# Starting the squared middle tiles and the block-product weights a few bytes into their SBUF buffers

## The chip, the cores and the metric

The kernel runs on one core of one Trainium2 chip. The metric is the device time of one execution, in microseconds. Before the change it is 1267.39 us, the median of three runs that lie between 1266.71 and 1267.39 us. One further execution was profiled, and every duration below comes from that one.

## The reference

The reference is a decoder trunk of two layers over 512 positions and 1024 channels, in float32. Each layer mixes positions with three parallel head groups (differential attention, a short gated convolution, RWKV-7) and then runs a squared-ReLU MLP. The change lies in the MLP alone:

```python
h = rms_norm(x, norm_mlp_g[l])
x = x + jnp.square(jax.nn.relu(h @ w_mlp_up[l])) @ w_mlp_down[l]
```

Here `w_mlp_up[l]` is 1024 x 4096 and `w_mlp_down[l]` is 4096 x 1024. After the last layer there is one more RMSNorm.

## The kernel before

Activations are held transposed: 128 channels on the partitions, 512 positions along the free dimension, so that one tile is 128 x 512 float32, 2048 bytes in each partition. Eight tiles make up the residual `x`.

To keep float32 accuracy with the fast `float32r` matmuls, every operand is split into a rounded part `hi` and a rest `lo`, and each product is made of three matmuls: `hi` by `hi`, `hi` by `lo` and `lo` by `hi`. ScalarE writes each `hi`, VectorE or GpSimd subtracts to get each `lo`. TensorE therefore issues, for each k of 128 channels, three weight loads and three matmuls. In a matmul the 128 x 128 weights are the operand that is loaded ahead (the stationary one), and the 128 x 512 or 128 x 256 activations are streamed through (the moving one).

The layer runs in stages. The first is the mixing stage, whose order of instructions is written out by hand; its last part, the output projection (`po` in the profile), takes `mhi` and `mlo` as moving operands. The second is the MLP, which lies in the `fp` pool of the layer and is emitted in plain program order:

- `up(i)` for the first 8 of 32 groups of middle channels (three of them are already done in the mixing stage): 24 matmuls of 512 columns each.
- `two(i0, i1)`, called 12 times a layer, does the other 24 groups in pairs by a scheme with 7 block products in the place of 8. Each product has 4 steps of k with 3 matmuls of 256 columns: 84 matmuls a call. The weights come as `raw` tiles or as their sums `s1` to `s4`, and `both` splits them into `shi` and `slo`, five buffers of each.
- `square` applies ReLU and the square, and `kept` splits the result into the middle tiles `mh` (ScalarE, line 1376) and `ml` (GpSimd, line 1377). They stand in rings of ten buffers each.
- `down(h, js)` multiplies four middle tiles by the down weights: for each output tile j, 12 matmuls of 512 columns with `mh` and `ml` as moving operands (`dn` in the profile). Between two calls of `two` stands half of such a group, 48 matmuls.
- In layer 1 the last quarter of the down projection is `last_group` (`dnF` in the profile): five output tiles with 24 matmuls of 512 columns, and three output tiles in two halves of 256 columns.

A matmul has two gates: its weights must be loaded and its moving operand written. The rings set how far ahead the other engines may work, and TensorE takes its work strictly in the order of the program.

Where tiles stand in a partition matters for what follows. The allocator rounds each buffer to a multiple of 32 bytes. In the program before, all middle tiles, all `shi` and `slo`, and the `thi`, `tlo`, `bhi` and `blo` activations start at a multiple of 64 bytes; the first middle tile, for example, at byte 98176. In the output projection the tiles are not all placed alike. The channel blocks are taken in the order 0, 5, 3, 1 (first four steps of `K_ORD`), and blocks 0 and 5 live in the mixing stage's own pool (`OWN`), while 3 and 1 live in the constant pool:

| moving tile of `po` | start byte in layer 0 | in layer 1 | past a multiple of 64 |
|---|---|---|---|
| `mhi`, `mlo` of block 0 | 210336, 212384 | 218528, 220576 | 32 |
| `mhi`, `mlo` of block 5 | 216480, 218528 | 212320, 214368 | 32 |
| `mhi`, `mlo` of block 3 | 35712, 37760 | 35712, 37760 | 0 |
| `mhi`, `mlo` of block 1 | 27520, 29568 | 27520, 29568 | 0 |

So each output tile of that projection's first part begins with six matmuls whose moving operand starts 32 bytes off, followed by six at a multiple of 64. Two kinds of weights are placed differently in the same way: `ksq`, the weights of the small `phsk` matmuls (128 x 128 weights, two columns streamed), stands 32 bytes off for the first two head pairs of layer 0 and at a multiple of 64 for the third.

A few elementwise outputs already start off a 32-byte multiple: `p[:, 1:]` at line 784 begins 4 bytes into its tile, `dx` written at line 906 starts 4 bytes past a multiple of 64, and `z[:, 2:]` at line 1220 begins 8 bytes into its tile.

Of the kernel before, what the change touches and what calls it, by code (L numbers as in the profile page):

```python
# [10 lines left out]
F32 = mybir.dt.float32  # L11
F32R = mybir.dt.float32r
# [10 lines left out]
S = 512  # L23
P = 128
# [255 lines left out]
def tile_trunk(ctx: ExitStack, tc: tile.TileContext, xT, wts, prm_d, cst_d, lora_d, gup_d, lam_d, fin_d, out):  # L280
# [25 lines left out]
    def psum(tag, bufs, name):  # L306
        return ps.tile([P, 512], F32, tag=tag, bufs=bufs, name=name)
# [177 lines left out]
    def last_group(fp, wbase, mids):  # L485


        g, H = N_KG - 1, S // 2
        mine = mids[8 * g:8 * g + 8]
# [18 lines left out]
        def norm(half, sq):  # L508
            q = slice(half * H, (half + 1) * H)
            pt = psum("rp", 4, f"pssF{half}")  # L510
            for i, a in enumerate((acc[:, q], sq)):
                for b in range(2):

                    pe.matmul(pt[:, b:b + 1], a[:, b * P:(b + 1) * P], ones1, start=(i == 0 and b == 0), stop=True,
                              skip_group_check=True)
            r = cp.tile([P, NB], F32, tag="rr", bufs=2, name=f"rrF{half}")
            for _ in rsqrt_act_steps(r[:, :2], pt[:, :2], 2, 1.0 / D, EPS):
                pass
            yield

            rb = [psum("rp", 4, f"prbF{half}_{i}") for i in range(1 + half)]
            for p in rb:
                for b in range(2):
                    pe.matmul(p[:, b * P:(b + 1) * P], r[:, b:b + 1].to_broadcast([P, P]), ident, start=True, stop=True)
            rbs = fp.tile([P, H], F32, tag="c0", bufs=2, name=f"rbs{half}")
            act.copy(rbs, rb[-1][:, :H])
            os_ = []
            for j in range(NK):
                o = fp.tile([P, H], F32, tag=("p1", "p5", "u2", "c1")[j // 2], bufs=2, name=f"o{half}_{j}")
                if j == 5 or j == 2 and not half:  # L530
                    pool.tensor_tensor(o, x[j][:, q], rbs, ALU.mult)
                else:
                    dve.tensor_tensor(o, x[j][:, q], rb[0][:, :H], ALU.mult)
                os_.append(o)
            for j in (0, 1, 3, 4, 2, 6, 5, 7):
                (nc.scalar if half and j in (1, 4, 6, 7) else nc.sync).dma_start(ov[j][:, q], os_[j])
            yield
# [34 lines left out]
    for l in range(L):  # L572
# [790 lines left out]
        with ExitStack() as mx:  # L1363
            fp = mx.enter_context(tc.tile_pool(name=f"fp{l}", bufs=1))
            RING = 10
            H = S // 2
            mids = []

# [2 lines left out]
            def kept(m):  # L1371

                i = len(mids)
                hi = fp.tile([P, S], F32R, tag="mh", bufs=RING, name=f"mh{l}_{i}")
                lo = fp.tile([P, S], F32R, tag="ml", bufs=RING, name=f"ml{l}_{i}")
                act.copy(hi, m)  # L1376
                pool.tensor_tensor(lo, m, hi.bitcast(F32), ALU.subtract)  # L1377
                mids.append((hi, lo))

            def square(cs, name):  # L1380

                r = fp.tile([P, S], F32, tag="r", bufs=2, name=f"r{name}")
                for i, c in enumerate(cs):
                    act.activation(r[:, i * H:i * H + c.shape[1]], c, AF.Relu)
                m = fp.tile([P, S], F32, tag="m", bufs=3, name=f"m{name}")
                act.activation(m, r, AF.Square)
                kept(m)
# [14 lines left out]
            bn, th = {}, {}  # L1402

            def scaled_by_norm(j):
                bn[j] = fp.tile([P, 2, H], F32, tag="shi" if j < 5 else "slo", bufs=5, name=f"bn{l}_{j}")
                dve.scalar_tensor_tensor(bn[j].rearrange("p a s -> p (a s)"), x[j], pr[:, C_GMLP + j:C_GMLP + j + 1], rb,
                                         ALU.mult, ALU.mult)

# [22 lines left out]
            def two(i0, i1):  # L1431

                n = f"{l}_{i0}"
                wg = wbase + NG_IN + NG_OUT

                def raw(i, a):
                    t = fp.tile([P, 4, P], F32, tag="sraw", bufs=6, name=f"raw{n}_{i}_{a}")
                    nc.sync.dma_start(t.rearrange("p k c -> p (k c)"), wts[wg + i, :, a * P:(a + 4) * P])
                    return t

                def both(src, name):
                    hi, lo = [fp.tile([P, 4, P], F32R, tag=f"s{p}", bufs=5, name=f"s{p}{n}_{name}") for p in ("hi", "lo")]
                    act.copy(hi, src)  # L1443
                    dve.tensor_tensor(lo, src, hi.bitcast(F32), ALU.subtract)  # L1444
                    return hi, lo

                def sum_(name, a, b, op):
                    t = fp.tile([P, 4, P], F32, tag=name, name=f"{name}{n}")
                    dve.tensor_tensor(t, a, b, op)
                    return t  # L1450

                def small(name):
                    return fp.tile([P, H], F32, tag=name, bufs=2, name=f"{name}{n}")

                def product(pt, w, moving, first=True):

                    whi, wlo = w
                    for k in range(4):
                        ahi, alo = moving(k)
                        pe.matmul(pt, whi[:, k], ahi, start=(first and k == 0), stop=False, skip_group_check=True)  # L1460
                        pe.matmul(pt, whi[:, k], alo, start=False, stop=False, skip_group_check=True)
                        pe.matmul(pt, wlo[:, k], ahi, start=False, stop=(k == 3), skip_group_check=True)

                blk = lambda d, q: lambda k: [p[:, q] for p in bs[4 * d + k]]
                smm = lambda q: lambda k: [p[:, q] for p in th[k]]
                pa, pb = [psum("rp", 4, f"p{i}{n}")[:, :H] for i in "ab"]
                pc = psum("at", 2, f"pc{n}")[:, :H]
                c0 = fp.tile([P, S], F32, tag="c0", bufs=2, name=f"c0{n}")
                w11 = raw(i0, 0)
                product(pa, both(w11, "p1"), blk(0, 0))  # L1470
                p1 = small("p1")
                act.copy(p1, pa)
                w21 = raw(i1, 0)
                w22 = raw(i1, 4)
                s1 = sum_("s1", w21, w22, ALU.add)
                product(pb, both(s1, "p5"), smm(0))
                p5 = small("p5")
                dve.tensor_copy(p5, pb)
                s2 = sum_("s2", s1, w11, ALU.subtract)
                product(pa, both(s2, "p6"), smm(1), False)  # L1480
                u2 = small("u2")
                act.copy(u2, pa)
                w12 = raw(i0, 4)
                product(pc, both(w12, "p2"), blk(1, 0))
                dve.tensor_tensor(c0[:, :H], pc, p1, ALU.add)
                s3 = sum_("s3", w11, w21, ALU.subtract)
                product(pa, both(s3, "p7"), smm(2), False)
                c1 = small("c1")
                dve.tensor_tensor(c1, pa, p5, ALU.add)  # L1489
                s4 = sum_("s4", w12, s2, ALU.subtract)  # L1490
                product(pb, both(s4, "p3"), blk(1, 1), False)
                dve.tensor_tensor(c0[:, H:], pb, u2, ALU.add)
                square([c0], f"{n}_0")
                product(pa, both(w22, "p4"), smm(3), False)
                square([pa, c1], f"{n}_1")
# [14 lines left out]
            for i in range(N_ONE):  # L1510
                up(i)
                for j in range(2 * max(i - 2, 0), min(2 * max(i - 1, 0), NK)):
                    scaled_by_norm(j)
                if i >= N_ONE - 4:
                    blocks(i - N_ONE + 4)
# [79 lines left out]
```

## Time and profile before

| what | value |
|---|---|
| median of three runs | 1267.39 us |
| the profiled execution's own time | 1266.47 us |
| its span, first to last instruction | 1264.7 us |
| TensorE matmul busy | 1242.8 us, 98% |
| VectorE, ScalarE, GpSimd busy | 72%, 55%, 27% |
| granted TensorE clock | 0.998 |
| matmuls `dn` (down projection), 512 columns | 3 x 448 |
| matmuls `dnF`, 512 and 256 columns | 3 x 40 and 3 x 48 |
| matmuls `pa`, `pb`, `pc` (block products), 256 columns | 2016 |

In the timeline each matmul has a start and a duration. The duration holds the whole trip through the array and overlaps with the next matmul's, so the cost of one matmul in a dense stream is read from the distance between successive starts, not from its duration. The windows view gives each engine's busy time in a stretch of the span, and the chain view lists the work that ended last, in order of time.

### The profile page before, as it was taken

The numbers are of one execution on the slowest core, as the hardware profiler recorded it, in microseconds if no ns is written. First come the engines' busy times: TensorE is split into PE (matmuls) and PEld (weight loads), VectorE is DVE, ScalarE is ACT, GpSimd is POOL, SyncE is SP. The second block draws the span as 40 slices with busy tenths as digits, with TensorE's granted clock in tenths as the row PEclk, the third lists the DMA queues.
The fourth block names the chain that finished last, engine by engine and source line by source line (L and its number), as shares of the span: only waits on it lengthen the run. The fifth ranks groups of instructions, "written<-read, shape, count | busy, mean of one in ns | idle before, by whom it ended". The sixth has DMA issues, their size and how long they took to land.

```text
span 1264.7 us, 25145 instructions
## 1 busy us (share of the span) xinstructions
PE 1242.8 (98%) x9493; PEld 1051.4 (83%) x9493; DVE 913.5 (72%) x1889; ACT 696.9 (55%) x1474; POOL 335.3 (27%) x433
## 2 busy tenths in 40 slices
PE   9999999999999999999999999999999999999997
PEld 6777777787789898989878787787787989898987
DVE  6788888867966666765667787879598666666654
ACT  7675655646744544544575656564575545454553
POOL 1353626133300101010224335352431010111110
PEclk9999999999999999999999999999999999999999
DMA  6522333142333333321235333332424233333122
GB/s 212 159 84 94 109 94 101 52 134 83 103 122 101 101 101 100 101 84 51 75 103 146 98 102 110 98 97 60 134 92 133 93 107 96 106 98 103 59 74 77
DMA packets 84410, 127.93 MB, mean 101 GB/s; under 512 B 21440, under 2 KB 25024, under 8 KB 84288
## 3 DMA queue, kind: packets, MB, share of 16 engines
q1 hardware_dynamic: 83568, 125.77, 32.6%
q8 instruction: 75, 1.23, 0.4%
q10 hardware_dynamic: 720, 0.55, 0.1%
q14 instruction: 47, 0.39, 0.1%
HBM read 117.11 MB, written 9.18 MB: 100 GB/s over the span
## 4 chain that ended last, share of the span: by engine, by line
PE 70%; DVE 4%; issue 1%; ACT 1%; DMA 0%; POOL 0%; DVEq 0%; ACTq 0%; POOLq 0%
PE dn L289 22%; PE pj L289 11%; PE pa L289 11%; PE up L289 6%; PE pb L289 5%; PE po L289 4%; PE dnF L289 3%; PE pc L289 3%; PE sc L289 1%; PE ptt L294 1%; PE pg L289 1%; DVE wlo L343 0%; DVE blo L1429 0%; DVE x L1505 0%; PE pyy L289 0%
## 5 line engine op out<-in xcount | busy, mean ns | idle before, releaser
L1377 POOL TENSOR_TENSOR ml<-m,mh 128x512 fp32r<-128x512 f32 x64 | 95.2, 1489 | 510.8 <-ACT mh L1376 510.6
L342 ACT CAST whi<-raw 128x512 fp32r<-128x512 f32 x142 | 88.1, 621 | 174.1 <-PE dn L289 158.5
L289 PE MATMUL dn<-mh,whi 128*128 128x512 f32 x448 | 175.3, 391 | 1.9 <-DVE x L1505 1.9
L289 PE MATMUL dn<-ml,whi 128*128 128x512 f32 x448 | 174.6, 390 | 0.0
L289 PE MATMUL dn<-mh,wlo 128*128 128x512 f32 x448 | 174.4, 389 | 0.0
L289 PE MATMUL pj<-ahim,whi 128*128 128x512 f32 x392 | 157.7, 402 | 4.4 <-DVE vf L1266 1.7
L289 PE MATMUL pj<-ahim,wlo 128*128 128x512 f32 x392 | 158.3, 404 | 0.0
L289 PE MATMUL pj<-alom,whi 128*128 128x512 f32 x392 | 158.2, 404 | 0.0
L662 ACT CAST whi<-raw 128x512 fp32r<-128x512 f32 x142 | 87.7, 619 | 93.6 <-PE pj L289 40.4
L671 POOL TENSOR_TENSOR wlo<-raw,whi 128x512 fp32r<-128x512 f32 x62 | 81.7, 1317 | 214.5 <-ACT whi L662 198.3
L1505 DVE TENSOR_TENSOR x<-dn,x 128x512 f32<-128x512 f32 x112 | 76.8, 686 | 76.8 <-PE dn L289 76.8
L343 DVE TENSOR_TENSOR wlo<-raw,whi 128x512 fp32r<-128x512 f32 x142 | 115.2, 812 | 11.4 <-ACT whi L342 10.7
L1444 DVE TENSOR_TENSOR slo_p<-s,shi_p 128x512 fp32r<-128x512 f32 x96 | 70.9, 740 | 63.6 <-ACT shi_p L1443 58.9
L289 PEld LDWEIGHTS dn<-mh,whi 128*128 128x128 f32 x448 | 84.2, 188 | 21.3 <-ACT whi L342 2.4
L289 PEld LDWEIGHTS dn<-mh,wlo 128*128 128x128 f32 x448 | 84.1, 188 | 17.8
L289 PEld LDWEIGHTS dn<-ml,whi 128*128 128x128 f32 x448 | 84.2, 188 | 16.5
L289 PEld LDWEIGHTS pj<-ahim,whi 128*128 128x128 f32 x392 | 73.9, 188 | 19.8 <-issue 1.7
L1443 ACT CAST shi_p<-s 128x512 fp32r<-128x512 f32 x96 | 59.2, 618 | 51.2 <-PE pa L289 39.1
L289 PEld LDWEIGHTS pj<-ahim,wlo 128*128 128x128 f32 x392 | 73.8, 188 | 14.3 <-issue 0.9
L289 PEld LDWEIGHTS pj<-alom,whi 128*128 128x128 f32 x392 | 73.8, 188 | 14.1 <-issue 0.5
L289 PE MATMUL pa<-thi,shi_p 128*128 128x256 f32 x288 | 81.6, 283 | 0.2 <-DVE c L1489 0.2
L289 PE MATMUL pa<-thi,slo_p 128*128 128x256 f32 x288 | 81.5, 283 | 0.0
(409 smaller groups left out, 3264.5 us busy)
## 6 DMA issues: line engine op xcount, KB each, us to landing
raw<-wts SPq DMA_DIRECT2D x391, 256.0 KB, 2.7
qs<-dqhi SPq DMA_DIRECT2D x24, 128.0 KB, 3.3
ks<-dkhi SPq DMA_DIRECT2D x24, 128.0 KB, 3.8
x<-xT SPq DMA_DIRECT2D x8, 256.0 KB, 5.0
dqhi<-qhi SPq DMA_DIRECT2D x6, 256.0 KB, 3.3
dqlo<-qlo SPq DMA_DIRECT2D x6, 256.0 KB, 2.8
dkhi<-khi SPq DMA_DIRECT2D x6, 256.0 KB, 2.6
dklo<-klo SPq DMA_DIRECT2D x6, 256.0 KB, 2.9
```

The costliest lines, as they stand in the source:

```text
L289: ins = nc.tensor.matmul(*a, **k)
L294: ins = nc.tensor.transpose(*a, **k)
L342: act.copy(hi[:, :n], raw[:, :n])
L343: (pool if a and lean[0] else dve).tensor_tensor(lo[:, :n], raw[:, :n], hi[:, :n].bitcast(F32), ALU.subtract)
L662: yield act.copy(hi[:, k0:k1], raw[:, k0:k1])
L671: yield eng.tensor_tensor(lo[:, :n], raw[:, :n], hi[:, :n].bitcast(F32), ALU.subtract)
L1377: pool.tensor_tensor(lo, m, hi.bitcast(F32), ALU.subtract)
L1443: act.copy(hi, src)
L1444: dve.tensor_tensor(lo, src, hi.bitcast(F32), ALU.subtract)
L1505: dve.tensor_tensor(x[j], pt, x[j], ALU.add)
```

## The change

The buffers of `mh`, `ml`, `shi`, `slo` and `bn` (which shares the buffers of `shi` and `slo`) grow from 512 to 544 elements, 128 bytes more in each partition. The middle tiles then use the 512 elements from element 4 (16 bytes) in layer 0 and from element 2 (8 bytes) in layer 1. The split block weights use those from element 4 (16 bytes) in layer 0 and from element 12 (48 bytes) in layer 1. `bn` still starts at element 0. No instruction is added or removed, no operand changes its shape, and the order stays the same. Because the larger buffers are all a multiple of 128 bytes longer, every other tile of the pool keeps its start relative to a multiple of 64.

```diff
             RING = 10
+            FROM, MID_FROM = ((4, 4), (12, 2))[l]
...
-                hi = fp.tile([P, S], F32R, tag="mh", bufs=RING, name=f"mh{l}_{i}")
-                lo = fp.tile([P, S], F32R, tag="ml", bufs=RING, name=f"ml{l}_{i}")
+                hi = fp.tile([P, S + 32], F32R, tag="mh", bufs=RING, name=f"mh{l}_{i}")[:, MID_FROM:MID_FROM + S]
+                lo = fp.tile([P, S + 32], F32R, tag="ml", bufs=RING, name=f"ml{l}_{i}")[:, MID_FROM:MID_FROM + S]
...
-                bn[j] = fp.tile([P, 2, H], F32, tag="shi" if j < 5 else "slo", bufs=5, name=f"bn{l}_{j}")
+                bn[j] = fp.tile([P, S + 32], F32, tag="shi" if j < 5 else "slo", bufs=5,
+                                name=f"bn{l}_{j}")[:, :S].rearrange("p (a s) -> p a s", s=H)
...
-                    hi, lo = [fp.tile([P, 4, P], F32R, tag=f"s{p}", bufs=5, name=f"s{p}{n}_{name}") for p in ("hi", "lo")]
+                    hi, lo = [fp.tile([P, S + 32], F32R, tag=f"s{p}", bufs=5,
+                                      name=f"s{p}{n}_{name}")[:, FROM:FROM + S].rearrange("p (k c) -> p k c", c=P) for p in ("hi", "lo")]
```

## The prediction

> **What bounds the kernel now.** I read the page first, from its busy times to the chain of work that ended last, then the windows of the two MLP stages, then the chain inside one of them, and last the timeline of single matmuls.
>
> ```profile
> PE 1242.8 (98%) x9493; PEld 1051.4 (83%) x9493; DVE 913.5 (72%) x1889; ACT 696.9 (55%) x1474; POOL 335.3 (27%) x433
> ...
> PE 70%; DVE 4%; issue 1%; ACT 1%; DMA 0%; POOL 0%; DVEq 0%; ACTq 0%; POOLq 0%
> PE dn L289 22%; PE pj L289 11%; PE pa L289 11%; PE up L289 6%; PE pb L289 5%; PE po L289 4%; PE dnF L289 3%; PE pc L289 3%; PE sc L289 1%; PE ptt L294 1%; PE pg L289 1%; DVE wlo L343 0%; DVE blo L1429 0%; DVE x L1505 0%; PE pyy L289 0%
> ```
>
> TensorE carries the chain, and the down projection (`dn`, `dnF`) and the block products (`pa`, `pb`, `pc`), whose operands the change moves, are its largest parts. The windows say whether anything else limits these stages.
>
> ```profile
> 345.00:600.00 255.00, 254.75 (x1594) 230.79 (x1593) 170.92 (x275) 120.49 (x231) 30.78 (x23) 1.00 0.31 96
> 965.00:1160.00 195.00, 195.00 (x1215) 176.60 (x1215) 133.76 (x216) 95.29 (x183) 23.67 (x18) 1.00 0.33 104
> ```
>
> After the length of the window the columns are TensorE matmul, weight loads, VectorE, ScalarE and GpSimd. In 255 us of layer 0 the matmuls leave 0.25 us free, in 195 us of layer 1 nothing, at a granted clock of 1.00. VectorE is free for 84 us and ScalarE for 135 us of the first window. So here the time is the number of matmuls times the distance between their starts, and only a change of that distance counts. The chain gives the rhythm:
>
> ```profile
> 1010.23 10.91 PE dn L289 x48
> 1021.14 1.43 PE pa L289 x12
> 1022.57 1.44 PE pb L289 x12
> ...
> 1031.21 8.87 PE dn L289 x39
> ```
>
> A period of 1031.21 - 1010.23 = 20.98 us is 48 `dn` matmuls in 10.91 us (227 ns each) and 84 block matmuls at 1.44 / 12 = 120 ns each. The single starts agree:
>
> ```profile
> 400.34 0.39 PE L289 MATMUL dn<-mh,whi 128*128 128x512 f32 x1
> ...
> 401.70 0.28 PE L289 MATMUL pa<-bhi,shi_p 128*128 128x256 f32 x1
> 401.81 0.28 PE L289 MATMUL pa<-blo,shi_p 128*128 128x256 f32 x1
> 401.93 0.28 PE L289 MATMUL pa<-bhi,slo_p 128*128 128x256 f32 x1
> ...
> 405.41 0.28 PE L289 MATMUL pa<-tlo,shi_p 128*128 128x256 f32 x1
> ```
>
> Six `dn` matmuls from 400.34 to 401.70 give 1.36 / 6 = 226.7 ns. The first of 256 columns behind them takes 0.11 us, all later ones 3.48 / 29 = 120 ns. Half of 226.7 would be 113.3: streaming alone would let the block products run at about 113, and something else, most likely the weight loads, holds them at 120. That matters for the weights below.
>
> **The change part by part.** Nothing is added or removed; four kinds of tiles start elsewhere. So there are three costs to find: `mh` and `ml` as the moving operand, `shi` and `slo` as weights, and the engines that write these tiles.
>
> *The moving operand.* How many matmuls read `mh` or `ml`:
>
> ```profile
> L289 PE MATMUL dn<-mh,whi 128*128 128x512 f32 x448 | 175.3, 391 | 1.9 <-DVE x L1505 1.9
> L289 PE MATMUL dn<-ml,whi 128*128 128x512 f32 x448 | 174.6, 390 | 0.0
> L289 PE MATMUL dn<-mh,wlo 128*128 128x512 f32 x448 | 174.4, 389 | 0.0
> ...
> L289 PE MATMUL dnF<-mh,whi 128*128 128x512 f32 x40 | 15.6, 389 | 0.0
> ...
> L289 PE MATMUL dnF<-mh,fhi 128*128 128x256 f32 x48 | 13.7, 286 | 0.0
> ```
>
> That is 3 x 448 + 3 x 40 = 1464 of 512 columns and 3 x 48 = 144 of 256. By the code 768 of the 1464 are in layer 0 (16 bytes) and 696 in layer 1 (8 bytes). No matmul before the change starts its moving operand at 8 or 16 bytes past a multiple of 64, but the output projection has one kind at 32: of each output tile's first twelve matmuls, six read blocks 0 and 5 (32 bytes off) and six read blocks 3 and 1 (at a multiple of 64). Layer 1:
>
> ```profile
> 880.47 0.40 PE L289 MATMUL po<-mhi,whi 128*128 128x512 f32 x1
> ...
> 881.87 0.40 PE L289 MATMUL po<-mhi,whi 128*128 128x512 f32 x1
> 882.10 0.39 PE L289 MATMUL po<-mlo,whi 128*128 128x512 f32 x1
> ...
> 883.24 0.40 PE L289 MATMUL po<-mhi,whi 128*128 128x512 f32 x1
> ```
>
> The six that start 32 bytes off run from 880.47 to 881.87, 1.40 / 6 = 233.3 ns each. Of the six aligned ones behind them the last five run from 882.10 to 883.24, 228 ns, which is 226.7 within the two digits shown. In layer 0:
>
> ```profile
> 257.49 0.39 PE L289 MATMUL po<-mhi,whi 128*128 128x512 f32 x1
> ...
> 258.88 0.40 PE L289 MATMUL po<-mhi,whi 128*128 128x512 f32 x1
> ...
> 260.28 0.39 PE L289 MATMUL po<-mhi,whi 128*128 128x512 f32 x1
> ...
> 261.66 0.40 PE L289 MATMUL po<-mhi,whi 128*128 128x512 f32 x1
> ```
>
> Here the six in the middle (258.88 to 260.28) are the unaligned ones, again 1.40 / 6 = 233.3 ns; the aligned six before and after take 1.39 / 6 = 231.7 and 1.38 / 6 = 230 ns. So 233.3 is stable, but what it is to be compared with is 226.7 in a settled stream and about 231 in a disturbed one. The price of an unaligned start lies between 233.3 - 231 = 2.3 and 233.3 - 226.7 = 6.6 ns by these rows. The `dn` streams are settled ones, so I take 6.7 ns (one thirty-fourth of 226.7). I take the same price at 16 and at 8 bytes: if the operand is fetched in aligned pieces of 64 bytes, any start within a piece touches one piece more, 33 for 32, whatever the offset. That is an inference from one offset. [...] A gain has no row: the fastest settled pace anywhere in the windows is the aligned 226.7.
>
> So 1464 x 6.7 ns = 9.8 us: 5.1 us in layer 0 and 4.7 us in layer 1, all on the path, as the windows show no idle time to absorb it. The 144 narrow ones would go from 113.3 to 120, the pace that already holds for 256 columns, so they count 0 (if that cover is gone, 144 x 6.7 ns = 1.0 us).
>
> *The weights.* 2016 block matmuls are held at 120 ns, so a longer or shorter load would show at once. The nearest rows are the small `phsk` matmuls, where two columns stream and the load of 128 x 128 weights is all there is; their weights start 32 bytes off at 45.16 and at a multiple of 64 at 143.44:
>
> ```profile
> 45.16 1.05 PE L289 MATMUL phsk<-cst,ksq 128*128 128x2 f32 x8
> 143.44 1.05 PE L289 MATMUL phsk<-cst,ksq 128*128 128x2 f32 x8
> ```
>
> Both groups of eight take 1.05 us, about 0.11 us a load. An unaligned start costs a load nothing there, so I take 0. The ends: a fetch price like that of the moving operand, 2016 x 6.7 ns = +13.5 us; or the loads get out of the way and the pace falls to 113.3, 2016 x 6.7 ns = -13.5 us.
>
> *The writers.* 64 `mh`, 64 `ml`, 168 `shi` and 168 `slo` are written at odd starts and read back once. Like shapes whose output begins 4 or 8 bytes into its tile:
>
> ```profile
> L784 DVE TENSOR_TENSOR pr<-pj,rsm 128x512 f32<-128x512 f32 x6 | 4.1, 686 | 1.6 <-PE pj L289 1.6
> ...
> L1213 DVE TENSOR_TENSOR uu<-pj,rsm 128x512 f32<-128x512 f32 x4 | 2.7, 681 | 0.0
> ...
> L1384 ACT ACTIVATE r<-c 128x512 f32<-128x512 f32 x40 | 25.3, 633 | 22.6 <-DVE c L1397 12.5 <-DVE c L1492 9.6
> ...
> L906 ACT ACTIVATE dx<-lw 128x512 f32<-128x512 f32 x6 | 3.8, 630 | 0.1
> ```
>
> VectorE takes 686 ns at 4 bytes (`pr`) and 681 at a multiple of 32 (`uu`); ScalarE 630 at 4 bytes (`dx`) and 633 aligned (`r`). I take 0. Even 5 ns on all 464 are 2.3 us, spread over engines with 84 us and more free. With TensorE slower the rings empty later, but the other engines keep their work ahead of it and DMA is busy 31% to 33%, so nothing new is late.
>
> *Sum.* 1266.47 us (the profiled execution) + 9.8 = 1276.3 us. That execution is 0.92 us below the median of the runs, so the median to expect is 1277.2 us.
>
> **The rivals.**
>
> *The weights pay as well.* For it: the pace of 120 shows that loads, not streaming, set the block products. Against it: the `phsk` pair. Time: 1277.2 + 13.5 = 1290.7 us.
>
> *Faster: the weights' new start frees the block products.* If loads and streaming hinder each other because both start at the same place relative to 64 bytes, a weight start of 16 or 48 bytes could bring the pace from 120 towards the 113.3 of the first matmul behind a `dn` run. With the middle tiles' 9.8 us still paid, the time is 1277.2 - 13.5 = 1263.7 us; it decides the sign from a pace below 120 - 9.8 us / 2016 = 115.1 ns. Against it: that first matmul has its weights loaded already during the longer one before, which explains 113.3 without any conflict.
>
> *Nothing happens.* The 16-byte start may be as good as an aligned one. [...] Against it: 32 bytes is a multiple of 16 too, and it ran at 233.3 ns. [...]
>
> *Only one layer pays,* the other offset being harmless: 1272 us.
>
> **How the numbers follow.** My forecast has a chance of 0.55, with a range of its own from 1271 (2.3 ns a matmul, 3.4 us) to 1280 us. The weights paying too has 0.12, faster 0.15, nothing 0.13, one layer 0.05. A measurement of this kernel tells about 0.2%, 2.5 us, from no change; so faster is 0.15, the same 0.13 and slower 0.55 + 0.12 + 0.05 = 0.72. The range from 1267 to 1291 takes in all but the faster case and a little of the outermost.
>
> **What would show it.** Right: `dn` starts 233 ns apart, 48 of them in 11.2 us, block products still 120 ns, a period of 21.3 us in both layers, and the rest of the span as before. Wrong: `dn` at 226.7 in either layer; block products at any pace but 120; layers that differ, which would tie the price to the offset; or gaps on TensorE in the two windows.

## The result and the profile after

The changed kernel takes 1271.13 us, the median of six runs between 1270.32 and 1273.0 us, against 1267.15 us before: 1.0033 times as long, with a 95% interval from 1.0023 to 1.0043. It is slower, by 4.0 us. The forecast was 1277.2 us, slower by 9.8 us: the direction holds, less than half of the amount came.

The profiled execution of the changed kernel took 1271.14 us, its span is 1269.3 us, 4.6 us more than before. From its page, busy times and chain:

```profile
PE 1247.0 (98%) x9493; PEld 1049.5 (83%) x9493; DVE 908.7 (72%) x1889; ACT 697.0 (55%) x1474; POOL 326.1 (26%) x433
...
PE 71%; DVE 3%; ACT 1%; issue 1%; DMA 0%; POOL 0%; DVEq 0%; ACTq 0%; POOLq 0%
```

The windows of the two MLP stages, columns as before:

```profile
345.00:600.00 255.00, 254.53 (x1585) 228.29 (x1584) 171.07 (x275) 120.70 (x231) 31.44 (x23) 1.00 0.31 96
965.00:1160.00 195.00, 195.00 (x1203) 174.27 (x1202) 131.00 (x217) 92.30 (x177) 18.52 (x17) 1.00 0.33 104
```

TensorE is as full as before and its clock as high (1.00 in both windows), but fewer matmuls fit: 1585 for 1594 in layer 0 and 1203 for 1215 in layer 1. So it is the distance of the starts again, and it grew more in layer 1. The chain shows by how much. Each line is a start, a length, and how many matmuls; the first five are in layer 0, the last four in layer 1:

```profile
497.02 11.09 PE dn L289 x48
508.11 1.42 PE pa L289 x12
509.53 1.41 PE pb L289 x12
...
518.03 11.09 PE dn L289 x48
529.12 1.42 PE pa L289 x12
...
1011.42 11.26 PE dn L289 x48
1022.69 1.42 PE pa L289 x12
...
1032.72 11.27 PE dn L289 x48
1053.98 11.03 PE dn L289 x47
```

| in one period | before | after, layer 0 | after, layer 1 |
|---|---|---|---|
| one `dn` matmul (length / 48) | 227.3 ns | 231.0 ns | 234.6 ns |
| one block matmul (rest of the period / 84) | 119.9 ns | 118.1 ns | 119.5 ns |
| the period | 20.98 us | 21.01 us | 21.30 us |

Two things were not in the main forecast: the block products became faster, and the two layers differ. The down projection costs 768 x 3.7 ns + 696 x 7.3 ns = 7.9 us more; the block products cost 1008 x 1.8 ns + 1008 x 0.4 ns = 2.2 us less by these periods. That leaves 5.7 us. Waits that went take back another 1.4 us. In the timeline of the kernel before, the third output tile of the first down projection of layer 1 waited for a PSUM bank that VectorE had still to add to `x`:

```profile
960.75 0.39 PE L289 MATMUL dn<-mh,wlo 128*128 128x512 f32 x1
962.10 0.47 PE L289 MATMUL dn<-mh,whi 128*128 128x512 f32 x1 [0.96 <-DVE x L1505]
```

From start to start that is 1.35 us for 0.23. In the changed kernel no such wait stands ahead of the third tile:

```profile
962.67 0.40 PE L289 MATMUL dn<-mh,wlo 128*128 128x512 f32 x1
962.91 0.39 PE L289 MATMUL dn<-mh,whi 128*128 128x512 f32 x1
```

With smaller waits at the next tiles, this first down projection loses 1.6 us before and 0.2 us after. It isn't the slower stream that covers the wait. In the first experiment below, whose `dn` matmuls are slower than before too (232 ns), the wait is still there:

```profile
964.64 0.47 PE L289 MATMUL dn<-mh,whi 128*128 128x512 f32 x1 [0.85 <-DVE x L1508]
```

What changed is the writer of `ml`. In layer 1, where the middle tiles start 8 bytes in, GpSimd's subtraction takes 1255 ns for 1510 (in layer 0, at 16 bytes, 1470 for 1469). Here is its line for layer 1, before and after:

```profile
L1377 POOL TENSOR_TENSOR ml<-m,mh 128x512 fp32r<-128x512 f32 x32 | 48.3, 1510 | 252.2 <-ACT mh L1376 251.9 <-POOL ml L1377 0.3
L1378 POOL TENSOR_TENSOR ml<-m,mh 128x512 fp32r<-128x512 f32 x32 | 40.2, 1255 | 262.1 <-ACT mh L1377 242.6 <-PE pa L289 18.6 <-POOL ml L1378 0.5
```

A subtraction of VectorE that takes 0.68 us otherwise can take much longer beside it. Four of them in the 25 us ahead of the wait (1.18 to 1.78 us before) are shorter by 0.2 us each, this one for example:

```profile
950.19 1.78 DVE L343 TENSOR_TENSOR wlo<-raw,whi 128x512 fp32r<-128x512 f32 x1
951.31 1.58 DVE L343 TENSOR_TENSOR wlo<-raw,whi 128x512 fp32r<-128x512 f32 x1
```

So VectorE finishes its addition 5.4 us after the stage's first `dn` matmul, not 6.4. In the experiments the wait is gone in the two other runs whose middle tiles start 8 bytes in, where `ml` takes 1255 and 1256 ns. In all others it is 0.95 to 1.12 us, but for one whose up projection is slower too (0.17 us).

By these terms the span should grow by 5.7 - 1.4 = 4.3 us. The 4.6 us measured have 0.6 us in them that the change did not cause: this execution's first `dn` matmul, ahead of which TensorE reads no moved tile, starts at 336.65 us, and at 336.08 us in the kernel before (at 59 us the matmuls are 0.8 us apart already). That makes 4.9 us for 4.6; the 0.3 us left over are about what paces read from single periods are good for.

### The profile page after: what moved, and what is told of

The parts are those of the page before. It is cut to its first block, busy times and chain, and to the rows that moved or that the text cites. A ratio compares the mean times of both kernels' runs of the same rounds, so it can differ in the third digit from the quotient of the medians.

```text
span 1269.3 us, 25145 instructions
## 1 busy us (share of the span) xinstructions
PE 1247.0 (98%) x9493; PEld 1049.5 (83%) x9493; DVE 908.7 (72%) x1889; ACT 697.0 (55%) x1474; POOL 326.1 (26%) x433
## 4 chain that ended last, share of the span: by engine, by line
PE 71%; DVE 3%; ACT 1%; issue 1%; DMA 0%; POOL 0%; DVEq 0%; ACTq 0%; POOLq 0%
PE dn L289 23%; PE pj L289 11%; PE pa L289 11%; PE up L289 6%; PE pb L289 5%; PE po L289 4%; PE dnF L289 3%; PE pc L289 3%; PE sc L289 1%; PE ptt L294 1%; PE pg L289 1%; PE pyy L289 0%; DVE x L1508 0%; DVE o L533 0%; DMA raw<-wts 0%
## 5 line engine op out<-in xcount | busy, mean ns | idle before, releaser
L1378 POOL TENSOR_TENSOR ml<-m,mh 128x512 fp32r<-128x512 f32 x64 | 87.1, 1362 | 521.5 <-ACT mh L1377 502.1
L343 DVE TENSOR_TENSOR wlo<-raw,whi 128x512 fp32r<-128x512 f32 x142 | 112.2, 790 | 11.8 <-ACT whi L342 11.8
L289 PE MATMUL pa<-tlo,shi_p 128*128 128x256 f32 x288 | 81.0, 281 | 0.0
```

The lines of the kernel that those rows point to most:

```text
L289: ins = nc.tensor.matmul(*a, **k)
L343: (pool if a and lean[0] else dve).tensor_tensor(lo[:, :n], raw[:, :n], hi[:, :n].bitcast(F32), ALU.subtract)
```

## The experiments

### Longer buffers with every start at zero

```diff
-            FROM, MID_FROM = ((4, 4), (12, 2))[l]
+            FROM, MID_FROM = ((0, 0), (0, 0))[l]
```

(Here and in the next three the base is the changed kernel.)

> The buffers grow by 128 bytes as in the change, but everything starts at their first byte. If the starts set the pace (start theory), the down projection is back at 227 ns a matmul of 512 columns in both layers and the block products at 120 ns, and the time is that of before, 1267.2 us. If the new spacing of the buffers (2176 bytes for 2048) set the pace (spacing theory), the down projection stays near 231 ns in layer 0 and 235 ns in layer 1, the block products near 118.4 and 119 ns, and the time is near 1271 us.

Measured: 1271.61 us, ratio to before 1.0036 (1.0022 to 1.0049), as slow as the change, without a single shifted start. In layer 1 the chain has

```profile
1013.07 11.15 PE dn L289 x48
1034.23 11.13 PE dn L289 x48
```

that is 232.1 ns a matmul; layer 0 gives 232.0 as the mean of its starts, and the block products 119.2 ns in both. So no start within a buffer is needed for the slower pace: the 128 bytes added to each buffer are enough. All starts here are at multiples of 64 bytes, so the theory that the prediction rested on, an extra 64-byte piece, doesn't explain it.

### Only the middle tiles, only the weights, other starts

Three more with longer buffers: only the middle tiles shifted, only the weights shifted, and other shifts.

```diff
+            FROM, MID_FROM = ((0, 4), (0, 2))[l]     # middle tiles alone
...
+            FROM, MID_FROM = ((4, 0), (12, 0))[l]    # weights alone
...
+            FROM, MID_FROM = ((8, 8), (2, 12))[l]    # other starts
```

> Only the middle tiles start later (16 bytes in layer 0, 8 bytes in layer 1). Start theory: the down projection at 231 and 235 ns as in the changed kernel, the block products at 120 ns; that is 768 x 3.6 ns + 696 x 7.6 ns = 8.1 us more than before, so about 1275 us, slower than the changed kernel. If the two parts did not act separately, the down projection would differ from 231 and 235 ns or the block products from 120 ns.

> Only the block products' weights start later (16 bytes in layer 0, 48 bytes in layer 1). Start theory: the down projection at 227 ns, the block products at 118.4 ns in layer 0 and 119.0 ns in layer 1, so 1008 x 1.5 ns + 1008 x 0.9 ns = 2.4 us less than before, about 1264.8 us: faster than both kernels. If the shorter pace of the block products came from the slower down projection between them (weights loaded further ahead), it is gone here: 120 ns and 1267.2 us.

> Other starts. Layer 0: middle tiles 32 bytes in, weights 32 bytes in. Layer 1: middle tiles 48 bytes in, weights 8 bytes in. If the price of the moving operand were one 64-byte piece more, as the prediction had it, the down projection runs at 233.3 ns in both layers. If the price is set by the start within a finer unit, so that 16 bytes costs 3.6 ns and 8 bytes 7.6 ns, then 32 bytes should cost no more than 16 did in the down projection (231 ns or less) and 48 bytes about the same. For the weights: if any start off a multiple of 64 helps, both layers stay near 118 to 119 ns; if only multiples of 16 bytes help, layer 1 is at 120 ns or above.

Measured, the paces as means over all matmul starts of a stage, waits left out:

| kernel | time (ratio to before) | `dn` layer 0, 1 | block products layer 0, 1 |
|---|---|---|---|
| middle tiles alone | 1271.69 us, 1.0039 (1.0024 to 1.0055) | 230.6, 235.0 ns | 119.0, 119.1 ns |
| weights alone | 1270.69 us, 1.0028 (1.0016 to 1.0039) | 232.1, 232.1 ns | 118.3, 118.7 ns |
| other starts | 1271.5 us, one run | 234.1, 232.5 ns | 118.7, 118.2 ns |

Weights alone were expected at 1264.8 us or 1267.2 us and came out slow, since the longer buffers of the middle tiles stayed. Middle tiles alone were expected near 1275 us with the block products at 120 ns; there too the longer buffers of the weights stayed, and the block products ran at 119. Neither expectation for the `dn` pace at other starts came (233.3 ns in both layers, or 231 or less). The starts do shift the pace (16 bytes a little below the 232 of zero, 8 bytes above it), but around a value that the spacing had already raised. A start at zero in a ring of 2176-byte buffers lies at 384, 0, 128 or 256 bytes modulo 512, from one buffer to the next. In the kernel before, every operand of these stages lies at 384 modulo 512, weights included. That suggests that the relative place of two operands counts, and the next runs ask for its period.

### Spacing of the middle tiles alone, by 128 and by 256 bytes

From here on the base is the kernel before; `shi`, `slo` and all other tiles stay at their places.

```diff
-                hi = fp.tile([P, S], F32R, tag="mh", bufs=RING, name=f"mh{l}_{i}")
+                hi = fp.tile([P, S + 32], F32R, tag="mh", bufs=RING, name=f"mh{l}_{i}")[:, :S]     # or S + 64
...
-                lo = fp.tile([P, S], F32R, tag="ml", bufs=RING, name=f"ml{l}_{i}")
+                lo = fp.tile([P, S + 32], F32R, tag="ml", bufs=RING, name=f"ml{l}_{i}")[:, :S]     # or S + 64
```

> The kernel before, with only the buffers of the middle tiles 128 bytes longer (2176 for 2048); the middle tiles start at their first byte and shi and slo stay where they were, so that of all TensorE operands only the middle tiles stand at several places modulo 512 bytes. Spacing theory, by way of the middle tiles: the down projection at 232 ns a matmul as with all buffers longer, the block products at 120 ns as before; 1464 x 4.7 ns = 6.9 us more than before less nothing, about 1274 us. If the spacing of shi and slo were needed too, the down projection stays at 227 ns and the time at 1267 us.

> The same with 256 bytes more (2304), so that the middle tiles stand at two places modulo 512 bytes and at one modulo 256. If what counts repeats every 256 bytes, the down projection is back at 227 ns and the time at 1267 us. If it repeats only every 512 bytes or more, it stays at 230 to 233 ns and the time is 1271 to 1275 us.

With 128 bytes more the time is 1274.65 us, ratio 1.0057 (1.0042 to 1.0072); in the chain 48 `dn` matmuls take

```profile
1015.13 11.13 PE dn L289 x48
1036.35 11.13 PE dn L289 x48
```

231.9 ns each, the block products stay at 119.9 ns. With 256 bytes more the time is 1267.32 us, ratio 1.0001 (0.9992 to 1.0011), and

```profile
1010.57 10.91 PE dn L289 x48
1031.55 10.91 PE dn L289 x48
```

227.3 ns. Both came as expected to a fraction of a us. So 256 bytes more from one buffer to the next changed nothing (227.3 ns), 128 bytes more did (231.9 ns). Spacing the middle tiles alone costs more than the whole change. The change's faster block products are missing here, but that is not all: in the profiled execution 1.4 us of the time lie in the mixing stage of layer 1, which reads none of the spaced tiles (323.1 us from the last `dn` of layer 0 to the first of layer 1, 321.8 us in both kernels).

In the first run the middle tiles stand at distance 0 from the weights and at 128 bytes in turn (modulo 256). The `dn` matmuls at distance 0 are as slow as the others, 233 ns against 231. So distance 0 alone doesn't give a `dn` matmul the 226.7 ns here, where its neighbours stand at 128.

### Whole groups shifted, spacing unchanged

An unused tile in the pool moves all that is allocated behind it; a second gap brings the rest back.

```diff
+            MID_AT, W_AT = ((128, 64), (256, 128))[l]    # second run: ((32, 256), (64, 32))[l]
+            def gap(n, name):
+                if n:
+                    fp.tile([P, n // 4], F32, tag=name, name=f"{name}{l}")
+            gap(MID_AT, "gap1")                          # ahead of the middle tiles
...
+                    gap((W_AT - MID_AT) % 512, "gap2")   # ahead of shi and slo
...
+                    gap(-W_AT % 512, "gap3")             # behind them
```

> All buffers keep their 2048 bytes; unused gaps shift whole groups of tiles. The middle tiles all stand 128 bytes (layer 0) or 256 bytes (layer 1) further modulo 512 than the down weights, and shi and slo 64 bytes (layer 0) or 128 bytes (layer 1) further than their moving operands. If the distance between a matmul's moving operand and its weights sets the pace, the down projection leaves 227 ns in one or both layers and the block products leave 120 ns. If only a change of place from one moving tile to the next costs, both stay at 227 and 120 ns, since within a stream all tiles stand at one place.

> The same with other distances: the middle tiles 32 bytes (layer 0) or 64 bytes (layer 1) further than the down weights, shi and slo 256 bytes (layer 0) or 32 bytes (layer 1) further than their moving operands. Distance theory: at 32 bytes the down projection runs at 233 ns, as the output projection's tiles that stand 32 bytes off did in the kernel before. If only a change of place within the stream costs: 227 ns and 120 ns everywhere.

The two took 1266.9 and 1272.23 us, one run each. A stream in which every matmul has the same distance can be slow too: `dn` 232.3 ns at 128 bytes, 227.6 at 256, 233.4 at 32, 229.0 at 64. So a change from one buffer to the next isn't needed for the slower pace. And the block products at 64 bytes ran at 114.5 ns, the best pace of any run so far. From the chain of the first of the two, layer 0:

```profile
496.39 11.14 PE dn L289 x48
507.54 1.39 PE pa L289 x12
508.93 1.36 PE pb L289 x12
510.29 1.36 PE pa L289 x12
```

1.36 / 12 = 113.3 ns, exactly half of 226.7.

### The change's starts without its spacing

```diff
-                hi = fp.tile([P, S + 32], F32R, tag="mh", ...)[:, MID_FROM:MID_FROM + S]
+                hi = fp.tile([P, S + 64], F32R, tag="mh", ...)[:, MID_FROM:MID_FROM + S]
```

and the same in `ml`, `bn`, `shi` and `slo`; the base is the changed kernel.

> The change with buffers 256 bytes longer instead of 128, so that all starts repeat modulo 256 bytes and only the starts themselves remain: middle tiles 16 bytes (layer 0) and 8 bytes (layer 1) further than the down weights, shi and slo 16 and 48 bytes further than their moving operands. Distance theory: each stream runs at one steady pace that differs from 227 and 120 ns; the pace at 16 and 8 bytes should lie between 227 ns (0) and 233.4 ns (32 bytes), the block products between 114.5 ns (64 bytes) and 120 ns. If the starts did nothing and the spacing was all, 227 and 120 ns and 1267 us.

Measured: 1270.79 us, ratio 1.0025 (1.0015 to 1.0035). `dn` runs at 231.6 ns at 16 bytes and 233.4 ns at 8 bytes:

```profile
497.48 11.12 PE dn L289 x48
518.53 11.12 PE dn L289 x48
...
1012.09 11.19 PE dn L289 x48
1033.27 11.23 PE dn L289 x48
```

The block products run at 118.3 and 118.8 ns. Here the forecast's price of 6.1 to 6.7 ns for layer 1 is nearly met (233.4 - 227.3 = 6.1), and layer 0 pays 4.3. The spacing alone and the starts alone each bring about what both bring together, so the costs don't add up. Either way the stream no longer stays at distance 0; why the costs don't add is not shown further.

### The weights' place against the moving operand's

Four runs ask which of the two places counts, and for a better one.

```diff
+            MID_AT, W_AT = ((0, 64), (0, 64))[l]          # shi, slo 64 bytes further
...
+            MID_AT, W_AT = ((192, 192), (96, 96))[l]      # other distances
...
-                    gap(-W_AT % 512, "gap3")              # as the first, but thi and tlo move along
...
+    wp.pool.tile([P, 16], F32, tag="gap0", bufs=1, name="gap0")   # all whi and wlo 64 bytes further,
+            MID_AT, W_AT = ((64, 0), (0, 0))[l]                   # middle tiles along in layer 0 only
```

> The kernel before with gaps that put shi and slo 64 bytes further modulo 256 than their moving operands in both layers, and nothing else moved. Distance theory: the block products at 114.5 ns as in layer 0 of the run with that distance, so 2016 x 5.4 ns = 10.9 us less than before, about 1256 us, faster than both kernels. If that pace was a side effect of the shifted middle tiles of that run, 120 ns and 1267 us.

> Further distances: middle tiles 192 bytes (layer 0) and 96 bytes (layer 1) further than the down weights; shi and slo 192 and 96 bytes further than their moving operands. If the sign of the distance does not matter, 192 bytes equals 64 bytes the other way: 229 ns and 114.5 ns. If what counts is how far the moving operand stands ahead of the weights, then shi and slo at 192 bytes are like middle tiles at 64: the block products stay near 120 ns, and the down projection at 192 bytes falls below 227 ns.

> Here shi, slo and also the sums of activation blocks (thi, tlo) stand 64 bytes further, while the plain activation blocks (bhi, blo) stay. If the distance between weights and moving operand sets the pace, the products with thi and tlo (distance 0) run at 120 ns and those with bhi and blo (distance 64) at 114.5 ns. If the weights' own place modulo 256 sets it, both kinds run at 114.5 ns.

> The kernel before with the weight buffers whi and wlo (all projections, the down projection too) 64 bytes further modulo 256. In layer 0 the middle tiles move along (distance 0 again, both at a new place), in layer 1 they stay (the weights stand 64 bytes further than the moving operand). Distance theory: the down projection at 227 ns in layer 0 and at 233 ns in layer 1 (the same distance as middle tiles 192 bytes further, which ran at 233.3). If the moving operand's own place sets the pace, layer 0 runs at 229 ns, as middle tiles shifted by 64 bytes did before, and layer 1 at 227 ns. The mixing stage's projections and the up projection, whose activations stay, show whether the same holds there: 233 ns against 227 in the up projection.

The first is faster than both kernels: 1262.85 us, ratio to before 0.9967 (0.9956 to 0.9979). Only the block products changed, to 117.8 ns, not to 114.5 ns; `dn` is untouched:

```profile
1008.03 10.91 PE dn L289 x48
1018.93 1.41 PE pa L289 x12
1020.35 1.41 PE pb L289 x12
```

So 2016 x 2.1 ns = 4.2 us less, where 10.9 were expected.

The second (1271.56 us, one run) has `dn` at 233.3 ns at both 192 and 96 bytes and the block products at 117.8 and 118.2 ns. Neither of its two expectations came for `dn`: 192 is not like 64 the other way (233.3 against 229.0), nor does it fall below 227. For the block products 192 is like 64 in the first run, 117.8 ns.

In the third (1263.76 us, one run), products with `thi` and `tlo` (distance 0) run at 119.5 and 118.9 ns, those with `bhi` and `blo` (distance 64) at 115.9 and 116.1 ns in layer 0, though all weights stand at the same place. So their own place alone doesn't set the pace: at one place of the weights the kind at distance 64 is about 3 ns faster than the kind at distance 0. That it runs at 116 ns and not at 114.5 may come from the change of kind after one or more products of 12 matmuls; no run shows that apart.

The fourth is the clearest; two more unused tiles, not shown, bring the rest back to its places. In layer 0 weights and middle tiles have moved together, in layer 1 the weights alone; the up projection has its weights moved and its activations not:

```profile
497.94 10.92 PE dn L289 x48
...
925.21 19.84 PE up L289 x85
...
1015.41 11.20 PE dn L289 x48
```

227.5 ns in layer 0, 233.3 ns in layer 1, and 19.84 / 85 = 233.4 ns in the up projection, whose chain before reads

```profile
920.75 24.29 PE up L289 x107
```

227.0 ns. It took 1275.0 us in one run, 7.9 us more than before. Both operands moved by 64 bytes leave the pace where it was (227.5 ns), the weights moved alone do not (233.3 ns), and the same shows in a stage that the change never touched (233.4 ns). So in these streams of 512 columns it was the distance that set the pace, not the place of one operand.

### Why 114 ns once and 118 ns another time

```diff
+            MID_AT, W_AT = ((32, 64), (64, 64))[l]
```

> shi and slo 64 bytes further than their moving operands in both layers, as in the fastest run, and besides the middle tiles 32 bytes (layer 0) and 64 bytes (layer 1) further than the down weights. If the block products' pace is a matter of their own distance alone, they stay at 117.8 ns in both layers. If it also depends on the state in which the down projection before them leaves the weight loads, they run near the 114.5 ns that they had behind middle tiles shifted by 128 bytes, in one or both layers.

Measured: 1268.55 us in one run. In layer 0, behind a `dn` stream at 233.3 ns, the block products stay at 117.7 ns; in layer 1, behind one at about 230 ns, they run at 113.4 ns:

```profile
1045.39 1.39 PE pa L289 x12
1046.78 1.36 PE pb L289 x12
1048.14 1.36 PE pa L289 x12
1049.50 1.36 PE pc L289 x12
```

The same distance thus has at least two steady paces. Which one comes goes with the stream in front: 113.3 behind middle tiles at 64 or 128 bytes, 117.8 behind those at 0 or 32. What it is that carries over stays open. The faster pace pays no more than the slower one does. From the first `dn` of layer 1 to the end of the span this execution takes 307.8 us, against 309.1 us before and 307.0 us in the fastest version. The `dn` matmuls give up 230 - 227.3 ns, and among the waits of TensorE's weight loads from 985 to 1200 us a new one stands, for VectorE's sum that must have read a PSUM bank before the last product adds to it:

```profile
PEld pa L289 <- DVE c L1500: 1.8, 7, 0.3
```

In the kernel before, with products of 120 ns, no wait of weight loads stands in that window.

The distances together, each from a run in which it was steady (middle tiles ahead of the down weights; `shi` and `slo` ahead of their moving operand):

| bytes modulo 256 | `dn`, 512 columns | block products, 256 columns |
|---|---|---|
| 0 | 227 ns | 120 ns |
| 8 | 233.4 | not measured alone |
| 16 | 231.6 | 118.3 |
| 32 | 233.4 | 118.3 |
| 48 | not measured alone | 118.8 |
| 64 | 229 to 230.7 | 113.4 or 117.8 |
| 96 | 233.3 | 118.2 |
| 128 | 232.3 | 120.1 |
| 192 | 233.3 | 117.8 |

## Why the prediction was right or wrong

**What bounds the kernel: right.** Both windows are still full, no other engine ended a wait worth naming inside them, and most of the effect is in the distance of matmul starts.

**The moving operand: the amount nearly right by luck, the reason wrong.** The term was 1464 x 6.7 ns = 9.8 us and came to 7.9 us, 3.7 ns in layer 0 and 7.3 ns in layer 1 where 6.7 was taken for both; that the layers differ was one of its signs of being wrong. The step that failed is "if the operand is fetched in aligned pieces of 64 bytes, any start within a piece touches one piece more". (One piece more on 32 would be 226.7 / 32 = 7.1 ns, not the 6.7 that the rows gave.) The rows of the output projection that it stands on were read rightly, 233.3 against 226.7 ns, but their tiles differ from the others in two ways, which one row can't part: they start 32 bytes past a multiple of 64, and they stand 32 bytes off their weights modulo 256. The second is enough by itself: with every start at a multiple of 64, `dn` took 232.3 ns at a distance of 128 bytes and 233.3 ns at 192. The buffers that grew by 128 bytes, which the prediction dismissed because starts stay at multiples of 64, cost as much by themselves as the shifted starts do.

**The weights: wrong.** "An unaligned start costs a load nothing there, so I take 0": the block products gained 2.2 us. The `phsk` pair (1.05 us for eight, wherever its weights stand) could not show it: it streams only two columns, and the gain came in products of 256. Part of the gain comes from the longer buffers, which with all starts at zero gave 119.2 ns. The range did hold this case. The faster rival supposed that loads and streaming get in each other's way by their relative place, and priced that at 13.5 us. Of the gain 2.2 us came, and the moving operand's 7.9 us outweighed it; that the pace depends on the relative place is measured, that loads are what holds it up is not shown. The objection to that rival, that the first block matmul is short merely because its weights are loaded already, does not hold as an objection: with another distance whole runs of products go at 113.3 ns each.

**What is hidden: one wait missed.** The text said the windows show no idle time to absorb anything. In layer 1 of the kernel before there were 1.6 us of waits at the first down projection, most of them ahead of the window's start at 965 us. A window must begin where the stage begins.

**The writers: wrong for one of them.** ScalarE and VectorE are busy 120.70 and 171.07 us in the first window, for 120.49 and 170.92 before, as the rows for their shapes said. For GpSimd, which writes `ml`, the prediction put 0 without any row. At 8 bytes its subtraction became 255 ns shorter (1255 for 1510), four of VectorE's subtractions beside it 0.2 us each, and 1.4 us of the waits just named went. A faster engine off the chain paid because it let another one finish sooner ahead of a wait.

**The other rivals.** "Nothing happens" is excluded by the interval (1.0023 to 1.0043). Nor is a start at 16 bytes as good as an aligned one: with the spacing undone a `dn` matmul takes 231.6 ns there, 4.3 ns more than before, and 6.1 ns more at 8 bytes.

**The sum.** 7.9 us for 9.8, less 2.2 for the 0 of the weights, less 1.4 for the 0 of the writers: 4.3 us, with 4.0 us in the medians (and 4.6 us in the spans, 0.6 of them from ahead of the moved tiles). That the time still lies in the main forecast's 1271 to 1280 us, at its lower edge, is luck: that range was made of other prices for the moving operand, not of the two gains that brought the time down there.

## What to carry to other kernels

With TensorE 98% busy the place of a tile was part of its cost here: `dn` matmuls took 227 ns at one distance between weights and moving operand and 233 ns at others. So compare the places of the two operands with each other, not each with a multiple of something, look whether that distance stays the same through a stream, and measure the pace from the starts of a long run of matmuls. Padding a buffer moves every later buffer of its ring: by 128 bytes it cost 0.4% to 0.6% of the time here, by 256 bytes nothing that could be measured (ratio 1.0001). In these runs the distance 0 was the best for streams of 512 columns (227 ns) and the worst, or nearly so, for 256 columns (120 ns; 120.1 at 128 bytes). When a row is taken as the price of a property, list in what else its tiles differ from the rest, and find a row for every engine that touches the moved tiles.

## What the runs showed of the hardware

In streams of one shape the pace of a float32r matmul changed with the distance between its two operands, from 226.7 to 233.4 ns at 512 columns and from 113.3 to 120 ns at 256. A distance of 256 bytes was like 0 (227.6 for 227.3 ns at 512 columns, 120 for 120 ns at 256), and so was a spacing of 2304 bytes for 2048 (227.3 ns). Why the distance counts is not shown.

The pace at 256 columns was not a function of the distance alone: at 64 bytes it was 113.4 ns behind one down projection and 117.7 ns behind another, in the same execution. Nor was the pace at 512 columns one of single matmuls: those at distance 0 took 233 ns in a stream that also has 128.

GpSimd's subtraction of 128 x 512 elements was faster with the subtrahend and the result 8 bytes past a multiple of 32 and the minuend not: 1255 or 1256 ns for 1510, in the three runs that have it. At 16, 32 and 48 bytes it was not (1470, 1468 and 1516 ns). Why is not shown.

The best version found is the kernel before with `shi` and `slo` 64 bytes further: 1262.85 us, 0.9967 of the time before (0.9956 to 0.9979).
